# Rests split engine by engine, an earlier low-rank load, thirteen bridging products, and output operands split at their groups

## The chip, the cores and the metric

The kernel runs on one core of one Trainium2 chip. The metric is the device time of one execution in microseconds (us); 904.47 us is the median of three runs of the kernel before (904.07, 904.47, 905.79). A profiled execution of it took 907.22 us, of which 905.4 us are the span that the trace shows. TensorE is called PE here, its weight loads PEld, VectorE DVE, ScalarE ACT, GpSimd POOL and SyncE SP.

## The reference

One encoder block on 512 tokens of width 2048: a normalisation modulated by a condition vector, one input projection whose columns feed two branches, dilated attention with 16 heads and gated linear attention (GLA) with 4 heads, a gate on each, one output projection, the residual and a last normalisation.

```python
mod = jax.nn.silu(c) @ w_cond[layer] + b_cond[layer]
shift, scale, gate = jnp.split(mod, 3, axis=-1)
h = rms_norm(x) * (1.0 + scale[:, None]) + shift[:, None]
proj = h @ w_in[layer]
aq, ak, av, ag, gq, gk, gv, gg, lr_f, lr_b = jnp.split(proj, PROJ_SPLITS, axis=-1)
...
log_g_f = (jax.nn.log_sigmoid((lr_f @ gla_gate_up_fwd[layer] + gla_gate_bias_fwd[layer]).astype(jnp.float32))
           / GLA_GATE_NORM).reshape(ks_)
...
y = jnp.concatenate([a_out, g_out], axis=-1) @ w_out[layer]
x = x + gate[:, None] * y
return rms_norm(x) * final_gain
```

The two low-rank columns `lr_f` and `lr_b` have rank 16 each. Everything is float32.

## The kernel before, in words

Every float32 operand is split into a high and a low part that PE takes at full speed: the high part is a copy by ACT (L493 for weights), the low part the difference by DVE (L477). A product is then three matmuls, high by high, low by high, high by low (`three`, L230 to L232). A weight arrives as a raw tile of 512 KB over SP's queue, is split, and is used.

PE goes through the program in this order. At the start it warms up (`warm`, L296), spreads the condition and warms again (L324) until the first product of stage a (`first_products`, L591) has its operands; stage a and stage b project the modulated tokens. From 187 to 440 us four units (qk2, qk4, qk6, gk) run with the attention of 16 heads beside them. A head has four tiles: `score` (two matmuls L839 and L840, the maximum on DVE L847, the exp on ACT L851, the reciprocal on DVE L854, a scaling on POOL L864), `turn` (transposes L882, the high part `pth` by ACT L888, the low part `ptl` by DVE L889), then `rest` for the edges that lie in 32 rows each (transpose L899, four copies by ACT L906, four differences by DVE L908) and `values` (L915: four matmuls with the high parts, then those with the low parts; its result goes to `oh` and `cat`, L922 and L926). A unit V (440 to 540 us) makes the GLA values by seven products of halves and holds the low-rank product and GLA head 0, whose output blocks `go` (L1123) read the masked scores `at` (L1108); four units for gates (ag0, ag1, gg0, gg1) hold heads 1 to 3. The output projection (744 to 897 us) is two pairs of seven products P1, P7, P6, P4, P5, P3, P2 of halves, each in four groups of weights. Their operands are sums and differences of the parts of `cat` (`to_s1`, `to_s2`, `to_s4`, L1471 to L1477) and their splits `c_h`, `c_l` (`halves`, L1458 and L1459). Some weights are sums of two raw tiles, added by DVE (L466).

The order on PE is written by hand: a unit places pieces of other work at given fractions of its length (the numbers beside a function, such as 0.7 or GLA_FIRST). The other engines take their instructions in the order that a scheduler makes of the program's order and of priorities; `tc.issue_after(x)` keeps a piece behind x. Every engine and each queue works in order, so an instruction that waits holds up what is behind it. A tile from a pool has a number of buffers, and a load into it waits until an old one is free: raw tiles of the output come from a pool of 3 (L396), raw V tiles (L391) wait for the buffer of a weight that has been split.

The low-rank weight `lrb` (256 KB) is loaded behind the unit gk (L1303), copied by ACT (L1306) and split by DVE (L1307) to `lrs`; the second factor `ups` is split at L1326.

Of the kernel before, what the change touches and what calls it, by code (L numbers as in the profile page):

```python
# [10 lines left out]
F32 = mybir.dt.float32  # L11
# [107 lines left out]
TOKENS = [slice(256 * c + a, 256 * c + 256, 2) for a in range(2) for c in range(2)]  # L119

GLA_AT = (0.01, 0.02, 0.33, 0.46, 0.46, 0.56, 0.64, 0.76, 0.76, 0.88)
GLA_FIRST = (0.3, 0.38, 0.55, 0.62, 0.775, 0.81, 0.86, 0.9, 0.92, 0.97)

SUMS_IN = {"ag0": 8, "ag1": 8, "gg0": 8}

# [66 lines left out]
def block_kernel(ctx: ExitStack, tc: tile.TileContext, a: dict):  # L192
# [15 lines left out]
    def T2(name, dt=F32, parts=P):  # L208
        return t2.tile([parts, 512], dt, tag="t2", name=name)
# [83 lines left out]
    def warm(n):  # L293

        for _ in range(n):
            mm(psw, hot[:, :P], hot, start=True, stop=True)  # L296
# [4 lines left out]
    with tc.manual_schedule(engines=PLANNED):  # L301
        small_inputs()
        cond_load(0, 0)
        half_load(0)
        x_load(0)
        half_load(1)
        nc.scalar.preload_act_table_set("silu_and_others")
        nc.vector.memset(hot.bitcast(F32), 1.0)
        nc.vector.memset(epst, EPS)
        nc.vector.memset(ch.bitcast(F32), 0.0)  # L310
        nc.vector.memset(sel.bitcast(F32), 0.0)
        nc.gpsimd.memset(cl.bitcast(F32), 0.0)
        warm(5)

        nc.vector.tensor_copy(ch[:4], cin[:, :512])
        act(sel[:4], cin[:, 512:], AF.Copy)
        tt(cl[:4], cin[:, :512], ch[:4].bitcast(F32), op=ALU.subtract)

        nc.vector.tensor_scalar(bcond[:, 16:32], bcond[:, 16:32], 1.0, None, op0=ALU.add)
        for j in range(4):  # L320
            spread(j, ch, True)
            spread(j, cl, False)
            act(sb[:, 512 * j:512 * j + 512], pcs[j], AF.Silu)
        warm(6)  # L324

    def cond_sum(dst, w, with_, init):

# [65 lines left out]

    def out_tile(s, name):
        if s % 2 and s >= OUT_DEEP:
            return op.tile([P, 2, 512], F32, tag="raw", bufs=3, name=name)  # L396
        return RAW(name, [2, 512])

    second = {}
# [418 lines left out]
    def attention(pairs):  # L818
# [77 lines left out]
        def rest(h):  # L896

            pk = PJ(f"r{h}")
            nc.tensor.transpose(pk[:, :P], pr_.pop((h, 0))[:, 0:128], ident)  # L899
            hi, lo = pts  # L900
            to = [(hi, 0, hi, 32), (hi, 0, lo, 0), (hi, 96, lo, 96), (hi, 64, hi, 96)]
            parts = [(t[a:a + 32, REST_OF[i], :], u[b:b + 32, REST_OF[i], :], pk[96 - 32 * i:128 - 32 * i, :P])
                     for i, (t, a, u, b) in enumerate(to)]
            for pair in (parts[:2], parts[2:]):
                for up, _, of in pair:
                    act(up, of, AF.Copy)  # L906
                for up, low_, of in pair:
                    tt(low_, of, up.bitcast(F32), op=ALU.subtract)  # L908

        def values(h):  # L910
            def go():
# [379 lines left out]
        for q in range(2):  # L1291
            qk_evict(p + 2 + q, ps[2 * q], ps[2 * q + 1])

    ps = unit("gk", False, attention((6, 7)))
    kp_.close()
    gs = mid.enter_context(tc.tile_pool(name="gs", bufs=1, reuse_waits="tile"))
    gla["k"] = B8("gkt", [4, 512])
# [1 line left out]
        act(gla["k"][:, i, :], ps[i], AF.Copy)  # L1299


    lrb = T2("lrb")
    nc.sync.dma_start(lrb.rearrange("p (k c) -> p k c", k=KT), a["w_lr"][0])  # L1303
    lrs = gp.tile([P, KT, 2, 32], F32R, tag="g", name="lrs")
    lrb3 = lrb.rearrange("p (k c) -> p k c", k=KT)
    act(lrs[:, :, 0, :], lrb3, AF.Copy)  # L1306
    tt(lrs[:, :, 1, :], lrb3, lrs[:, :, 0, :].bitcast(F32), op=ALU.subtract)  # L1307
    plr = PA("plr")
# [161 lines left out]
    def to_s1(z):  # L1470
        tt(part(z, 1), part(2 + z, 1), part(z, 1), op=ALU.subtract)  # L1471
# [9 lines left out]
            (0.65, lambda: to_s1(0)), (0.8, lambda: to_s2(0))]  # L1481
    ps = unit("gg1", False, side + some_sums("gg1"))
    gate_evict(ps, cat[3], "g1")
    to_s1(1)
    to_s2(1)
    mid.close()
    op = ctx.enter_context(tc.tile_pool(name="op", bufs=1, reuse_waits="tile"))
    for e in "hl":
# [145 lines left out]
    def later(pair, prod, g, go):  # L1634
        todo.setdefault((pair, prod, g), []).append(go)

    def product(pair, prod, ps, first, last, rows=(0, 1)):

        ah, al = ops[with_[prod]]
        for g in range(4):  # L1640
            s = (pair * len(OUT_ORDER) + OUT_ORDER.index(prod)) * 4 + g
            i0 = gi["O", s]
            ahead = 0 in rows
            if ahead:
                split_hi(i0)
                split_hi(i0 + 1)
                for n in (2, 3, 4, 5):
                    fetch(i0 + n)
                whole(i0 + 2)
                split_lo(i0)  # L1650
                for go in todo.get((pair, prod, g), ()):
                    go()
            wh, wl = wts[i0]
            for n in rows:
                t = slice(P * n, P * n + P)
                for kk in range(2):
                    k = 2 * g + kk
                    c = slice(512 * kk, 512 * kk + 512)
                    three(ps[n], ah[:, k, t], al[:, k, t], wh[:, c], wl[:, c],
                          first and k == 0, last and k == 7, not first)  # L1660
                if ahead and n == 0:
                    split_lo(i0 + 1)

    def a12():
        operand("A12", [B8(f"A12{e}", [4, 512], F32R) for e in "hl"])

    for z in range(2):
        later(0, "P1", 2 * z, halves("S2", z, part(z, 0)))
        later(0, "P7", 2 * z, halves("A22", z, part(2 + z, 1)))
        later(0, "P6", 2 * z, halves("S1", z, part(z, 1)))  # L1670
        later(0, "P6", 2 * z + 1, lambda z=z: (to_s4(z), halves("S4", z, part(z, 0))()))
    later(0, "P4", 0, a12)
    for z in range(2):
        later(0, "P4", 1 + 2 * z, lambda z=z: halves("A12", z, part(2 + z, 0))())
# [133 lines left out]
```

## Time and profile before

| what | us |
|---|---|
| runs, median (lowest, highest) | 904.47 (904.07, 905.79) |
| profiled execution | 907.22 |
| its span | 905.4 |
| PE busy in the span | 890.0 (98%) |
| DVE busy | 731.2 (81%) |
| ACT busy | 491.6 (54%) |
| POOL busy | 125.9 (14%) |
| DMA read from and written to memory, over the span | 305 GB/s |

A row of the timeline gives the start in the span, the time, the engine, the line, the operation, what it writes and reads, and in brackets how long the engine had been idle before it and what ended that. Matmuls overlap, so a matmul of 0.39 us does not hold up the next for as long; the starts tell the pace. The row of a DMA on SP is its issue, not its landing.

### The profile page before, as it was taken

How to read it: one execution, taken by the hardware profiler on the slowest of the kernel's cores; microseconds unless marked ns; L12 is line 12 of the kernel's file. 1: busy time of each engine (PE TensorE's matmuls, PEld its weight loads, DVE VectorE, ACT ScalarE, POOL GpSimd, SP SyncE). 2: the span in 40 equal slices, each digit the busy share in tenths (PEclk: the TensorE clock that was granted, in tenths of full speed). 3: DMA queues.
4: the chain of work that ended last, by engine and by line, in shares of the span. 5: the costliest groups of instructions: out<-in, count | busy, mean ns of one | idle time of the engine just before them, and what ended most of it. 6: DMA issues, size and time to landing. Idle time of an engine off the chain costs nothing.

```text
span 905.4 us, 12339 instructions
## 1 busy us (share of the span) xinstructions
PE 890.0 (98%) x4159; PEld 739.2 (82%) x4159; DVE 731.2 (81%) x1220; ACT 491.6 (54%) x841; POOL 125.9 (14%) x219
## 2 busy tenths in 40 slices
PE   8999999999999999999999999999999999999996
PEld 6888788888888888887778888888888888888885
DVE  7998799878989989888568668595787559797687
ACT  5554533466655745655657554373664248455454
POOL 0000000023323333243000101112020100000001
PEclk9999999999999999999999999999999999999999
DMA  9999489398798898998778879778796988777863
GB/s 342 401 411 363 186 344 367 134 306 226 202 266 273 247 265 247 249 298 223 232 260 255 311 206 308 206 249 262 231 279 208 275 286 289 282 288 249 289 238 154
DMA packets 65547, 242.33 MB, mean 268 GB/s; under 512 B 9190, under 2 KB 11526, under 8 KB 55883
## 3 DMA queue, kind: packets, MB, share of 16 engines
q1 hardware_dynamic: 58724, 199.23, 61.5%
q0 software_dynamic: 6464, 42.01, 19.4%
q8 instruction: 33, 0.54, 0.2%
q10 hardware_dynamic: 296, 0.30, 0.1%
q14 instruction: 30, 0.25, 0.1%
HBM read 224.64 MB, written 51.47 MB: 305 GB/s over the span
## 4 chain that ended last, share of the span: by engine, by line
PE 91%; DVE 3%; ACT 2%; DMA 2%; issue 1%; SPq 0%; DVEq 0%; ACTq 0%
PE ps_qk L230 5%; PE ps_qk L232 5%; PE ps_qk L231 5%; PE g L232 4%; PE g L230 4%; PE g L231 4%; PE stb L232 3%; PE stb L231 3%; PE stb L230 3%; PE ps_ag L232 3%; PE ps_ag L230 3%; PE ps_ag L231 3%; PE o L915 3%; PE sta L230 3%; PE sta L231 3%; PE sta L232 3%
## 5 line engine op out<-in xcount | busy, mean ns | idle before, releaser
L864 POOL TENSOR_SCALAR p<-p,st 128x32 f32<-128x32 f32 (+2 forms) x108 | 59.8, 565 | 159.9 <-DVE st L854 91.2
L328 DVE CUSTOM_DVE_ANT_0 cb<-cb,sb,c_bcond 128x2048 f32<-128x2048 f32 (+1 forms) x32 | 73.4, 2295 | 1.9 <-DMA cb<-in_wm 1.6
L851 ACT ACTIVATE p<-p,st 128x416 f32<-128x416 f32 x64 | 41.0, 641 | 49.2 <-DVE st L847 42.3
L429 POOL DMA_DIRECT2D T<-in_w_o x32 | 23.2, 725 | 159.4 <-ACT V2h L493 14.8
L888 ACT ACTIVATE pth<-t 128x384 fp32r<-128x384 f32 x64 | 31.0, 485 | 19.8 <-PE t L882 11.1
L889 DVE TENSOR_TENSOR ptl<-t,pth 128x384 fp32r<-128x384 f32 x64 | 35.2, 551 | 5.2 <-ACT pth L888 3.7
L882 PE MATMUL t<-c_ident,p 128*128 128x128 f32 x192 | 31.3, 272 | 0.0
L882 PEld LDWEIGHTS t<-c_ident,p 128*128 128x128 f32 x192 | 24.3, 139 | 7.9
L847 DVE CUSTOM_DVE_ANT_0 p<-s,g,st 128x256 f32<-128x256 f32 x64 | 27.7, 432 | 1.8
L847 DVE CUSTOM_DVE_ANT_0 p<-s,g 128x160 f32<-128x160 f32 x64 | 23.5, 367 | 4.2 <-PE s L840 3.5
L328 DVE CUSTOM_DVE_ANT_0 rawg<-rawg,crow,gate 128x1024 f32<-128x1024 f32 x16 | 20.4, 1279 | 4.0 <-DMA rawg<-in_wg 4.0
L1581 POOL TENSOR_SCALAR x<-x,rn 128x512 f32<-128x512 f32 x2 | 2.3, 1167 | 148.5 <-ACT rn L1570 148.5
L429 POOL DMA_DIRECT2D T3V<-in_w_gv x8 | 5.5, 687 | 125.1 <-ACT qk21h L493 118.7
L839 PE MATMUL s<-ks,qh 128*128 128x416 f32 x64 | 22.6, 353 | 0.0
L906 ACT ACTIVATE pth<-r 32x128 fp32r<-32x128 f32 x64 | 17.2, 269 | 9.9 <-PE r L899 4.5
L840 PE MATMUL s<-ks,ql 128*128 128x416 f32 x64 | 22.4, 350 | 0.0
L1091 ACT ACTIVATE sq<-st,sc 128x256 f32<-128x256 f32 x24 | 12.2, 506 | 18.6 <-DVE st L1081 10.0
L328 DVE CUSTOM_DVE_ANT_0 rawg<-rawg,crow,c_bcond 128x1024 f32<-128x1024 f32 x16 | 20.3, 1279 | 0.5 <-DVE g L1028 0.5
L429 POOL DMA_DIRECT2D T<-T x16 | 9.1, 571 | 79.9 <-ACT V8h L493 12.9
L915 PE MATMUL o<-pth,vv 128*128 128x512 f32 (+1 forms) x64 | 15.9, 369 | 2.2 <-DVE pth L908 1.1
L466 DVE TENSOR_TENSOR raw_O<-raw_O,raw_P 128x1024 f32<-128x1024 f32 x8 | 9.8, 1225 | 10.1 <-DMA raw_O<-in_w_o 7.8
L568 ACT ACTIVATE h_hi<-xt,shift 128x512 fp32r<-128x512 f32 x16 | 11.5, 721 | 10.3 <-DVE shift L328 9.5
(1661 smaller groups left out, 3151.6 us busy)
## 6 DMA issues: line engine op xcount, KB each, us to landing
cb<-in_wm SPq DMA_DIRECT2D x31, 1024.0 KB, 9.3
T<-in_w_o POOLq DMA_DIRECT2D x32, 512.0 KB, 6.5
rawg<-in_wg SPq DMA_DIRECT2D x32, 512.0 KB, 5.4
raw_O<-in_w_o SPq DMA_DIRECT2D x32, 512.0 KB, 4.6
raw_qk<-in_w_qk SPq DMA_DIRECT2D x24, 512.0 KB, 4.9
raw_O<-T SPq DMA_DIRECT2D x24, 512.0 KB, 5.0
rawb<-in_w_sb SPq DMA_DIRECT2D x16, 512.0 KB, 8.9
rawv<-in_wv SPq DMA_DIRECT2D x16, 512.0 KB, 5.6
```

The source lines that it names most:

```text
L230: mm(ps, lh, rh, start=first, stop=False, skip_group_check=more)
L231: mm(ps, ll, rh, start=False, stop=False, skip_group_check=more)
L232: mm(ps, lh, rl, start=False, stop=last, skip_group_check=more)
L328: return nc.vector.tensor_tensor_reduce(out=w, in0=w, in1=with_, op0=ALU.mult, op1=ALU.add, scale=1.0, scalar=init, accum_out=dst)
L429: move = nc.gpsimd.dma_start(dst, src, max_dma_last_dim=8192, **how).ins
L847: top = nc.vector.tensor_tensor_reduce(out=t[:, lo:hi], in0=ps[:, lo:hi], in1=gt[h][:, at:at + 2 * (hi - lo) - 1:2], op0=ALU.add, op1=ALU.min,
L851: act(t, t, AF.Exp, bias=st[:, 0:1], scale=-1.0, accum_out=st[:, 1:2])
L864: last["pool"] = nc.gpsimd.tensor_scalar(to, of, st[:, 2:3], 1.0, op0=ALU.mult, op1=ALU.mult).ins
L882: nc.tensor.transpose(pk[:, n_ * P:n_ * P + P], t[:, first_ + kt * P:first_ + kt * P + P], ident)
L888: act(hi, src, AF.Copy)
L889: tt(lo, src, hi.bitcast(F32), op=ALU.subtract)
L915: mm(po[:, P * a0:P * a1], vv[h // 4][:, c, h % 4, :], pt[:, at:at + (a1 - a0 - 1) * step + 1:step, :], start=n_ == z == 0, stop=False, sk ...
```

## The change

It has six parts. The second warm-up has 13 matmuls in place of 6. In `rest` ACT makes all four copies before DVE makes the four differences, where before it was two and two. The low-rank load is issued within the unit gk, at 0.7 of its length, and no longer behind it. In the output, `to_s1` and `to_s2` of the second half are moved from before the output into the groups 2 and 3 of P1, and the sums and splits of the operands are placed in the order of the weights' splits by the new function `in_turn`; the split of S2 goes to group 1 of P1 and of P7 from groups 0 and 2 of P1. The pool of raw tiles in the output has four buffers. Two of the numbers of GLA_FIRST, 0.9 and 0.92, are 0.91 and 0.93.

```diff
@@ -119,7 +119,7 @@
 TOKENS = [slice(256 * c + a, 256 * c + 256, 2) for a in range(2) for c in range(2)]
 
 GLA_AT = (0.01, 0.02, 0.33, 0.46, 0.46, 0.56, 0.64, 0.76, 0.76, 0.88)
-GLA_FIRST = (0.3, 0.38, 0.55, 0.62, 0.775, 0.81, 0.86, 0.9, 0.92, 0.97)
+GLA_FIRST = (0.3, 0.38, 0.55, 0.62, 0.775, 0.81, 0.86, 0.91, 0.93, 0.97)
 
 SUMS_IN = {"ag0": 8, "ag1": 8, "gg0": 8}
 
@@ -321,7 +321,7 @@
             spread(j, ch, True)
             spread(j, cl, False)
             act(sb[:, 512 * j:512 * j + 512], pcs[j], AF.Silu)
-        warm(6)
+        warm(13)
 
     def cond_sum(dst, w, with_, init):
 
@@ -393,7 +393,7 @@
 
     def out_tile(s, name):
         if s % 2 and s >= OUT_DEEP:
-            return op.tile([P, 2, 512], F32, tag="raw", bufs=3, name=name)
+            return op.tile([P, 2, 512], F32, tag="raw", bufs=4, name=name)
         return RAW(name, [2, 512])
 
     second = {}
@@ -901,11 +901,10 @@
             to = [(hi, 0, hi, 32), (hi, 0, lo, 0), (hi, 96, lo, 96), (hi, 64, hi, 96)]
             parts = [(t[a:a + 32, REST_OF[i], :], u[b:b + 32, REST_OF[i], :], pk[96 - 32 * i:128 - 32 * i, :P])
                      for i, (t, a, u, b) in enumerate(to)]
-            for pair in (parts[:2], parts[2:]):
-                for up, _, of in pair:
-                    act(up, of, AF.Copy)
-                for up, low_, of in pair:
-                    tt(low_, of, up.bitcast(F32), op=ALU.subtract)
+            for up, _, of in parts:
+                act(up, of, AF.Copy)
+            for up, low_, of in parts:
+                tt(low_, of, up.bitcast(F32), op=ALU.subtract)
 
         def values(h):
             def go():
@@ -1291,7 +1290,13 @@
         for q in range(2):
             qk_evict(p + 2 + q, ps[2 * q], ps[2 * q + 1])
 
-    ps = unit("gk", False, attention((6, 7)))
+    lrb = []
+
+    def lr_load():
+        lrb.append(T2("lrb"))
+        nc.sync.dma_start(lrb[0].rearrange("p (k c) -> p k c", k=KT), a["w_lr"][0])
+
+    ps = unit("gk", False, attention((6, 7)) + [(0.7, lr_load)])
     kp_.close()
     gs = mid.enter_context(tc.tile_pool(name="gs", bufs=1, reuse_waits="tile"))
     gla["k"] = B8("gkt", [4, 512])
@@ -1299,10 +1304,8 @@
         act(gla["k"][:, i, :], ps[i], AF.Copy)
 
 
-    lrb = T2("lrb")
-    nc.sync.dma_start(lrb.rearrange("p (k c) -> p k c", k=KT), a["w_lr"][0])
     lrs = gp.tile([P, KT, 2, 32], F32R, tag="g", name="lrs")
-    lrb3 = lrb.rearrange("p (k c) -> p k c", k=KT)
+    lrb3 = lrb[0].rearrange("p (k c) -> p k c", k=KT)
     act(lrs[:, :, 0, :], lrb3, AF.Copy)
     tt(lrs[:, :, 1, :], lrb3, lrs[:, :, 0, :].bitcast(F32), op=ALU.subtract)
     plr = PA("plr")
@@ -1481,8 +1484,6 @@
             (0.65, lambda: to_s1(0)), (0.8, lambda: to_s2(0))]
     ps = unit("gg1", False, side + some_sums("gg1"))
     gate_evict(ps, cat[3], "g1")
-    to_s1(1)
-    to_s2(1)
     mid.close()
     op = ctx.enter_context(tc.tile_pool(name="op", bufs=1, reuse_waits="tile"))
     for e in "hl":
@@ -1633,6 +1634,14 @@
 
     def later(pair, prod, g, go):
         todo.setdefault((pair, prod, g), []).append(go)
+
+    def in_turn(pair, prod, g, *fns):
+
+        def go():
+            with tc.issue_after(last["hi"]), tc.issue_after(last["lo"]):
+                for fn in fns:
+                    fn()
+        later(pair, prod, g, go)
 
     def product(pair, prod, ps, first, last, rows=(0, 1)):
 
@@ -1664,11 +1673,13 @@
     def a12():
         operand("A12", [B8(f"A12{e}", [4, 512], F32R) for e in "hl"])
 
+    in_turn(0, "P1", 2, lambda: to_s1(1))
+    in_turn(0, "P1", 3, lambda: to_s2(1))
     for z in range(2):
-        later(0, "P1", 2 * z, halves("S2", z, part(z, 0)))
-        later(0, "P7", 2 * z, halves("A22", z, part(2 + z, 1)))
-        later(0, "P6", 2 * z, halves("S1", z, part(z, 1)))
-        later(0, "P6", 2 * z + 1, lambda z=z: (to_s4(z), halves("S4", z, part(z, 0))()))
+        in_turn(0, ("P1", "P7")[z], 1, halves("S2", z, part(z, 0)))
+        in_turn(0, "P7", 2 * z, halves("A22", z, part(2 + z, 1)))
+        in_turn(0, "P6", 2 * z, halves("S1", z, part(z, 1)))
+        in_turn(0, "P6", 2 * z + 1, lambda z=z: to_s4(z), halves("S4", z, part(z, 0)))
     later(0, "P4", 0, a12)
     for z in range(2):
         later(0, "P4", 1 + 2 * z, lambda z=z: halves("A12", z, part(2 + z, 0))())
```

On DVE, around the rest of attention head 13 (`r` is its transposed tile; L908 in the old and L907 in the new are its differences, `t` a turned tile, `gk7l` the low part of the last weight of the unit gk). Before:

```order
L908 TENSOR_TENSOR pth<-r_4040,pth 32x128
L908 TENSOR_TENSOR ptl<-r_4040,pth 32x128
L889 TENSOR_TENSOR ptl<-t_4050,pth 128x3x128
L847 ISA p_4063,st_4064<-s_4060,g_3867 128x160
L847 ISA st_4064 128x1
L477 TENSOR_TENSOR gk7l<-raw_gk_3978,gk7h 128x1024
L847 ISA p_4063,st_4064<-s_4060,g_3867,st_4064 128x256
L847 ISA st_4064 128x1
L908 TENSOR_TENSOR ptl<-r_4040,pth 32x128
L1243 TENSOR_TENSOR S_4001<-S_4001,h_lo 128x512
L908 TENSOR_TENSOR pth<-r_4040,pth 32x128
```

Now (the first of the four L907 stands three rows further up):

```order
L907 TENSOR_TENSOR ptl<-r_4047,pth 32x128
L847 ISA p_4070,st_4071<-s_4067,g_3874,st_4071 128x256
L847 ISA st_4071 128x1
L907 TENSOR_TENSOR ptl<-r_4047,pth 32x128
L1242 TENSOR_TENSOR S_4008<-S_4008,h_lo 128x512
L907 TENSOR_TENSOR pth<-r_4047,pth 32x128
L854 RECIPROCAL st_4071<-st_4071 128x1
L889 TENSOR_TENSOR ptl<-t_4057,pth 128x3x128
L847 ISA p_4102,st_4103<-s_4099,g_3874 128x256
L847 ISA st_4103 128x1
L477 TENSOR_TENSOR gk7l<-raw_gk_3985,gk7h 128x1024
```

The turn's L889 and the split gk7l stood ahead of the last two differences and stand behind them now.

On ACT, the copy `lrs` and what stands around it, before at the end of head 15:

```order
L1299 ACTIVATE gkt<-ps_gk_3671 128x512
L888 ACTIVATE pth<-t_4277 128x3x128
L1299 ACTIVATE gkt<-ps_gk_3672 128x512
L888 ACTIVATE pth<-t_4286 128x3x128
L906 ACTIVATE pth<-r_4296 32x128 x2
L1306 ACTIVATE lrs<-lrb 128x16x32
L888 ACTIVATE pth<-t_4306 128x3x128
L906 ACTIVATE pth<-r_4296 32x128 x2
```

and now at the first tile of head 15, whose exp is the L851 behind it:

```order
L921 ACTIVATE oh_4127<-o_4115 64x512
L888 ACTIVATE pth<-t_4138 128x3x128
L1309 ACTIVATE lrs<-lrb 128x16x32
L851 ACTIVATE p_4152,st_4153<-p_4152,st_4153 128x416
L888 ACTIVATE pth<-t_4171 128x3x128
L493 ACTIVATE V0h<-raw_V_4083 128x1024
```

The copy has moved from between two turns of the last head to a place 35 rows further up, ahead of an exp, and on SP the load stands between the raw V tiles 4 and 5.

On DVE at the beginning of the output (`O2l` is the low part of the third weight, `c_l` that of an operand). Before:

```order
L1202 TENSOR_TENSOR cat_5990<-cat_5990,sgg_6774 128x512
L1202 TENSOR_TENSOR cat_5990<-cat_5990,sgg_6777 128x512
L1202 TENSOR_TENSOR cat_5990<-cat_5990,sgg_6780 128x512
L1459 TENSOR_TENSOR c_l<-cat_1611,c_h 128x1024
L1202 TENSOR_TENSOR cat_5990<-cat_5990,sgg_6783 128x512
L1477 TENSOR_TENSOR cat_1611<-cat_5127,cat_1611 128x4x256
L1471 TENSOR_TENSOR cat_3027<-cat_5990,cat_3027 128x4x256
L477 TENSOR_TENSOR O2l<-raw_O_6807,O2h 128x1024
```

Now:

```order
L1201 TENSOR_TENSOR cat_5997<-cat_5997,sgg_6781 128x512
L1201 TENSOR_TENSOR cat_5997<-cat_5997,sgg_6784 128x512
L1201 TENSOR_TENSOR cat_5997<-cat_5997,sgg_6787 128x512
L1201 TENSOR_TENSOR cat_5997<-cat_5997,sgg_6790 128x512
L477 TENSOR_TENSOR O2l<-raw_O_6812,O2h 128x1024
L1462 TENSOR_TENSOR c_l<-cat_1618,c_h 128x1024
L1474 TENSOR_TENSOR cat_3034<-cat_5997,cat_3034 128x4x256
L477 TENSOR_TENSOR O3l<-raw_O_6814,O3h 128x1024
```

The third weight's low part stands ahead of the operand's low part and of the sums, of which one (the old L1477) has gone behind the low parts of weights 4 to 9.

## The prediction

> **What bounds the kernel now.** I read the waits of TensorE (PE) first: what it waited for, us in total, times, longest.
>
> ```profile
> PE sta L591 <- ACT h_hi L534: 2.7, 1, 2.7
> ...
> PE o L915 <- DVE pth L908: 1.1, 1, 1.1
> PE o L915 <- ACT pth L888: 1.0, 1, 1.0
> ```
>
> PE sets the time, and what an edit elsewhere can bring is one of these few waits, some tenths that hide between matmuls, or a slow clock. So I looked for clock next, in the table of stretches (length, busy us of PE, of its weight loads, DVE, ACT, POOL, then the clock granted, DMA share, GB/s):
>
> ```profile
> 7.86:11.28 3.42, 1.03 (x5) 0.84 (x6) 2.82 (x6) 2.23 (x5) 0.00 (x0) 1.00 1.03 406
> 11.28:14.69 3.41, 3.41 (x10) 2.64 (x9) 2.31 (x3) 1.00 (x2) 0.00 (x0) 0.50 1.03 429
> ...
> 895.33:898.74 3.41, 1.59 (x7) 0.97 (x6) 2.31 (x6) 2.23 (x6) 0.99 (x1) 1.00 0.26 102
> 898.74:902.15 3.41, 0.00 (x0) 0.00 (x0) 2.10 (x5) 2.01 (x6) 0.00 (x0) 1.00 0.78 310
> ```
>
> After a stretch in which PE was busy for 30% (1.03 of 3.42) the clock was half for 3.41 us. After one of 47% (1.59 of 3.41, at the end) it stayed full. So the 2.7 us wait of the start costs a second time: 3.41 us at half clock lose about 1.7 us of matmuls.
>
> Each wait below is read from starts: a matmul of 512 columns starts 0.23 us after the one before it while nothing holds it up, as the rows of 790.67 and 791.13 show further down, two starts apart.
>
> **The change, part by part.** *Seven more matmuls at the start.* Six stand there and fill nothing that is on the path. Thirteen last 7 x 0.23 = 1.6 us longer, and the hole is 2.7 us, so the first product still waits only for its operand; about 1.1 us stay idle. In the worst place of a 3.41 us stretch PE is then busy for (3.41 - 1.1)/3.41 = 68%, over the 47% that kept the clock. What is late next is the split operands:
>
> ```profile
> 21.20 0.74 DVE L537 SCALAR_TENSOR_TENSOR h_lo<-xt,scale,h_hi 128x512 fp32r<-128x512 f32 x1
> ...
> 23.10 0.39 PE L231 MATMUL sta<-sa2hi,h_lo 128*128 128x512 f32 x1
> ```
>
> This low half is ready at 21.94 and used at 23.10, so of 1.7 us at most 1.15 survive. Against the profiled execution the edit is worth 1.1. Against the median it is worth less if the stretches lie otherwise there. The hole is 2.65 us; if a stretch needs between 1.8 us of it (busy 47%) and 2.4 us (busy 30%) to lose the clock, and stretches of 3.41 us begin anywhere, between (0.76 + 2 x 0.25)/3.41 = 37% and (0.76 + 2 x 0.85)/3.41 = 72% of the executions pay. About half: 0.55. Bounds 0 and 1.1.
>
> [...]
>
> *The rests engine by engine.* In head 13 the DVE rows are (start, us):
>
> ```profile
> 413.74 0.29 DVE L908 TENSOR_TENSOR pth<-r,pth 32x128 fp32r<-32x128 f32 x1 [0.17 <-ACT pth L906]
> ...
> 414.36 0.56 DVE L889 TENSOR_TENSOR ptl<-t,pth 128x384 fp32r<-128x384 f32 x1
> ...
> 415.20 1.22 DVE L477 TENSOR_TENSOR gk7l<-raw_gk,gk7h 128x1024 fp32r<-128x1024 f32 x1
> ...
> 417.89 0.28 DVE L908 TENSOR_TENSOR pth<-r,pth 32x128 fp32r<-32x128 f32 x1
> ```
>
> ```profile
> 416.82 0.40 PE L232 MATMUL ps_gk<-h_lo,gk5h 128*128 128x512 f32 x1
> 418.32 1.05 PE L915 MATMUL o<-pth,vv 128*128 128x512 f32 x4 [1.10 <-DVE pth L908]
> ```
>
> PE was free at 417.05 and started at 418.32, 0.15 behind the last L908 (its end, 418.17): 1.27 lost. In the new order the L889 and the split gk7l stand behind all four L908. The four copies of ACT now come first, two of them more at 0.28 each, so the first L908 goes from 413.74 to 414.3; two L908 take 0.6; from 414.36 to 418.17 it took 3.8, less 0.56 and 1.22 that moved behind, 2.0. The last ends at 416.9 to 417.1, PE starts at 417.1 to 417.25, and **1.05 of the 1.27 is gained**. Behind it queue L889, needed only by the low products some 0.9 us later, and gk7l, which now ends near 414.3 + 2.6 + 0.56 + 0.5 + 1.22 = 419.3 (one score piece of 0.5 ahead of it) in place of 416.4. The other heads have no such wait, and the same 0.57 of delay costs them at most a tenth each; I take 0 for these.
>
> *The low-rank load.* Now (SP, ACT, PE):
>
> ```profile
> 434.49 0.64 SPq L1303 DMA_DIRECT2D lrb<-in_w_lr  x1
> ```
> ```profile
> 435.91 0.60 ACT L1299 ACTIVATE gkt<-ps_gk 128x512 f32<-128x512 f32 x1
> ...
> 437.78 0.55 ACT L906 ACTIVATE pth<-r 32x128 fp32r<-32x128 f32 x2
> 441.12 0.63 ACT L1306 ACTIVATE lrs<-lrb 128x512 fp32r<-128x512 f32 x1 [2.78 <-DMA lrb<-in_w_lr]
> 441.77 0.49 ACT L888 ACTIVATE pth<-t 128x384 fp32r<-128x384 f32 x1
> ...
> 443.36 1.05 ACT L1326 ACTIVATE ups<-upr 128x1024 fp32r<-128x1024 f32 x1
> ```
> ```profile
> 440.92 0.39 PE L232 MATMUL ps_gv_P<-V0l,h_hi 128*128 128x512 f32 x1
> 442.31 1.13 PE L915 MATMUL o<-pth,vv 128*128 128x512 f32 x4 [1.01 <-ACT pth L888]
> ```
>
> The copy lrs holds the last turn of head 15 on ACT, and PE, free at 441.15, starts 1.16 later. With lrs gone from there, ACT has from 435.91 on two gkt (0.5 each by their starts), three L888 (0.49), the four copies (1.1) and ups (1.05), which moves ahead: 4.6 us, to 440.5. That is before 441.15, so the wait ends; a further 0.1 goes in the low products behind it. **1.2 gained.**
>
> But lrs needs a new place. On SP the load stands behind the fourth raw V tile, which waits for the buffer of gk7l: 419.3, with its own issue of 0.64 about 419.9. It is moved past three loads and a store there; the raw V tile now behind it goes 0.64 later, far ahead of its use. On ACT lrs stands between the turn of head 14's second tile and the exp of head 15's first. When does it land? Nearest rows (KB, us from issue to landing), the load itself as it was, and a raw V tile alone, from the stretch 419 to 427:
>
> ```profile
> lrb<-in_w_lr SPq DMA_DIRECT2D x1, 256.0 KB, 6.6
> ```
> ```profile
> raw_V<-in_w_gv SPq DMA_DIRECT2D x1, 512.0 KB, 3.1
> ```
>
> So 423.0 to 426.5. The stretch is quieter than the one at 434, but a tile of 512 KB goes out just ahead: I take 424.0. The exp behind it waits for its maximum:
>
> ```profile
> 423.60 0.48 DVE L847 CUSTOM_DVE_ANT_0 p<-s,g,st 128x256 f32<-128x256 f32 x1
> ```
> ```profile
> 424.00:429.00 5.00, 5.00 (x28) 4.24 (x27) 4.90 (x15) 3.66 (x9) 0.61 (x1) 1.00 0.58 187
> ```
>
> That maximum is there at 424.08, so lrs (0.63) costs ACT nothing if the load lands by 423.45, and each microsecond later delays exp, reciprocal, turn and the next score by as much. And DVE has no room here, 4.90 of 5.00 busy: its half of lrs (0.69, as long as its 128x512 kin at 417) and the wait for two more copies of ACT (0.57) are not hidden: 1.26. At 424.0 the price is 1.26 + 0.55 = **1.8 lost**, at PE's turns and scores of head 15's last tiles. Bounds: 0.7 (early, and PE's slack of about half a microsecond there used) and 1.26 + 3.05 = 4.3.
>
> *The outputs of GLA head 0 one product later.*
>
> ```profile
> 524.30 0.69 DVE L1108 SCALAR_TENSOR_TENSOR at<-c_ident,at 128x512 f32<-128x512 f32 x1
> ```
> ```profile
> 524.46 0.39 PE L232 MATMUL ps_gv_P<-V25l,vS 128*128 128x512 f32 x1
> 525.13 0.46 PE L1123 MATMUL go<-at,gv 128*128 128x128 f32 x2 [0.28 <-ACT V27h L493]
> ```
>
> PE, free at 524.69, waits for `at`, which ends at 524.99 and is taken at 525.13: 0.44. Three matmuls more ahead of it (0.68) cover that. What is later next is the rest of head 0's chain, so I take **0.35 gained** between 0 and 0.5.
>
> *The output's operands at their groups, and a fourth raw tile.*
>
> ```profile
> 744.87 1.23 DVE L1459 TENSOR_TENSOR c_l<-cat,c_h 128x1024 fp32r<-128x1024 f32 x1 [0.90 <-ACT c_h L1458]
> ...
> 746.61 1.22 DVE L1477 TENSOR_TENSOR cat<-cat,cat 128x1024 f32<-128x1024 f32 x1
> 747.75 1.22 DVE L1471 TENSOR_TENSOR cat<-cat,cat 128x1024 f32<-128x1024 f32 x1
> 748.88 1.22 DVE L477 TENSOR_TENSOR O2l<-raw_O,O2h 128x1024 fp32r<-128x1024 f32 x1
> ```
> ```profile
> 749.63 0.39 PE L231 MATMUL g<-O2h,A11l 128*128 128x512 f32 x1
> 750.15 0.50 PE L232 MATMUL g<-O2l,A11h 128*128 128x512 f32 x1
> ```
>
> PE reaches O2l's product at 749.86 and starts at 750.15, and 0.1 more goes right behind: 0.4. In the new order O2l stands ahead of the first three rows, over 3 us earlier. **0.4 gained.** The moved work, two halves c_l and an addition of 1.2 each, comes up again between 771 and 791, where DVE has room only because it waits for a tile:
>
> ```profile
> 782.53 1.22 DVE L466 TENSOR_TENSOR raw_O<-raw_O,raw_P 128x1024 f32<-128x1024 f32 x1 [3.17 <-DMA raw_O<-in_w_o]
> ...
> 789.35 1.22 DVE L477 TENSOR_TENSOR O17l<-raw_O,O17h 128x1024 fp32r<-128x1024 f32 x1
> ```
> ```profile
> 790.67 0.39 PE L230 MATMUL g<-O17h,c_h 128*128 128x512 f32 x1
> ...
> 791.13 0.39 PE L232 MATMUL g<-O17l,c_h 128*128 128x512 f32 x1
> ```
>
> O17l ends 0.56 before its use. The hole of 3.17 us at 782.5 takes two of the three pieces; the third, and two additions that now stand ahead of O17l, must find the tiles earlier, which the fourth raw tile allows. I cost it at nothing; if that cover fails, one piece of 1.2 less 0.56 is 0.7 lost, and all three are 3.1.
>
> **The sum.** 1.05 + 1.2 + 0.35 + 0.4 - 1.8 = 1.2 gained, and the start 0.55 against the median, 1.1 against the profiled execution. That one took 907.22 us, 905.4 in the span and 1.8 around it, 2.75 over the median of 904.47; by the sum it becomes 904.9. The median becomes 904.47 - 1.75 = **902.7 us**.
>
> **Rivals.** *The load lands late.* The gains without it are 3.0, so the whole change is slower from the moment when 1.26 + (landing - 423.45) exceeds 3.0: landing after 425.2. With its old 6.6 us it lands at 426.5: 4.3 lost, 905.8 with nothing from the start, 905.2 with its half. The old row speaks for it, the 3.1 of the raw tile against. Over 427 it is slower by 1.8.
>
> *The start in full, and an early load.* If the median runs had the half clock and the load lands by 423: 3.0 - 0.7 + 1.1 = 3.4, **901.1**. For it: the three runs lie 1.7 us apart, about what the half clock costs.
>
> *The start brings nothing:* the runs of the median had full clock anyway, and 904.47 - 1.2 = **903.3**. For it: the profiled execution, which had half clock, is the slowest of all. [...]
>
> *A new wait in the output.* O17l stands behind two additions that wait for tiles: 0.7 to 3.1 lost, **904.6** in the middle (1.9). For it: the hole is a DMA wait, not spare time. Against: one more tile to fetch ahead.
>
> **How the numbers follow.** A measurement of this kernel tells 0.2%, 1.8 us, from no change: faster is below 902.66. The forecast (load between 423 and 425, the start by half) has 0.42, half of it on either side of that limit: 0.22 faster, 0.20 same. Full start and early load 0.20, faster. No start 0.14: 0.03 faster, 0.11 same. Late load 0.13: 0.08 same, 0.05 slower. New output wait 0.11: 0.06 same, 0.05 slower; it takes the remainder of reorderings that I can't price. Sum: faster 0.45, same 0.45, slower 0.10; I move 0.02 from same to slower since the order of DVE changes in hundreds of rows. The range goes from 900.0 (all bounds on the good side: 3.0 - 0.7 + 1.1 + the 0.15 of GLA and a microsecond for tiles that come earlier) to 905.6 (late load, half start, 0.4 over).
>
> **What would show it.** Clock 1.00 throughout from 5 us on, and no half stretch; if the first half low operand is then waited for at 21.9, the 1.15 holds. No wait over 0.3 us at the o of heads 13 and 15, none at go and at O2l's product. In exchange waits of some 1.8 us in all at turns and scores of head 15 between 424 and 431, and lrs on ACT near 424. Wrong would be: lrb landing past 425.5, a wait at O15l to O20l near 780 to 795, or a wait of the same size at head 13's o, which would mean that the four L908 still stand behind other work on DVE.

## The result

The changed kernel takes 906.44 us (median of 14 runs, 905.90 to 907.75), the kernel before in the same comparison 905.11 us (14 runs, 904.07 to 908.57). The ratio is 1.0016, 95% interval 1.0009 to 1.0023: the change makes it slower by about 1.4 us. The forecast was 902.7 us in a range of 900.0 to 905.6. It has the wrong sign, and the time lies outside the range.

The profiled executions tell the opposite at first sight: 906.70 us with a span of 904.9, against 907.22 with 905.4. Both readings are right, since the profiled execution of the kernel before was 2.1 us longer than its median and that of the changed one only 0.26. What follows has to account for both.

### The profile page after: what moved, and what is told of

It is laid out like the page before. It is cut to its first block, busy times and chain, and to the rows that moved or that the text cites. A ratio compares the mean times of both kernels' runs of the same rounds, so it can differ in the third digit from the quotient of the medians.

```text
span 904.9 us, 12332 instructions
## 1 busy us (share of the span) xinstructions
PE 891.7 (99%) x4166; PEld 739.2 (82%) x4166; DVE 730.7 (81%) x1220; ACT 491.7 (54%) x841; POOL 126.7 (14%) x219
## 4 chain that ended last, share of the span: by engine, by line
PE 48%; DVE 3%; ACT 1%; issue 1%; DMA 1%; DVEq 0%; SPq 0%; ACTq 0%
PE g L231 4%; PE g L232 4%; PE g L230 4%; PE ps_ag L230 3%; PE ps_ag L231 3%; PE ps_ag L232 3%; PE ps_gv_P L231 3%; PE ps_gv_P L230 3%; PE ps_gv_P L232 3%; PE ps_gg L232 2%; PE ps_gg L231 2%; PE ps_gg L230 2%; PE go L1122 2%; PE gx L231 2%; PE gx L232 2%; PE gx L230 2%
## 5 line engine op out<-in xcount | busy, mean ns | idle before, releaser
L851 ACT ACTIVATE p<-p,st 128x416 f32<-128x416 f32 x64 | 41.0, 641 | 56.6 <-DVE st L847 44.8
L889 DVE TENSOR_TENSOR ptl<-t,pth 128x384 fp32r<-128x384 f32 x64 | 35.0, 550 | 3.1 <-ACT pth L888 2.3
L847 DVE CUSTOM_DVE_ANT_0 p<-s,g,st 128x256 f32<-128x256 f32 x64 | 27.6, 432 | 1.7
L847 DVE CUSTOM_DVE_ANT_0 p<-s,g 128x160 f32<-128x160 f32 x64 | 23.6, 369 | 4.5 <-PE s L840 3.8
L839 PEld LDWEIGHTS s<-ks,qh 128*128 128x128 f32 x64 | 12.0, 188 | 7.7 <-issue 1.9
L1358 DVE TENSOR_TENSOR vS<-rawS,vS 128x1024 fp32r<-128x1024 f32 x8 | 9.7, 1223 | 9.5 <-ACT vS L1357 9.4
```

Source lines behind the costliest of these rows:

```text
L839: mm(ps[:, :NK], qh[:, q], ks[:, k], start=True, stop=False)
L847: top = nc.vector.tensor_tensor_reduce(out=t[:, lo:hi], in0=ps[:, lo:hi], in1=gt[h][:, at:at + 2 * (hi - lo) - 1:2], op0=ALU.add, op1=ALU.min,
L851: act(t, t, AF.Exp, bias=st[:, 0:1], scale=-1.0, accum_out=st[:, 1:2])
L889: tt(lo, src, hi.bitcast(F32), op=ALU.subtract)
```

## The profile after

The waits of TensorE (PE) in the changed kernel (us in total, times, longest):

```profile
PE s L839 <- DVE st L847: 1.8, 4, 1.0
PE warm L296 <- DVE hot L308: 1.5, 1, 1.5
PE sta L591 <- ACT h_hi L534: 0.7, 1, 0.7
PE t L882 <- DVE st L847: 0.5, 1, 0.5
```

The waits of the old list that the change aimed at are gone or shorter: the 2.7 us at the start are 0.7, and the two at `o` and the one at `go` don't appear. In their place stands a wait that the old list does not have: scores `s`, and one turn `t`, that wait for the maximum on DVE (L847).

The start, in the table of stretches (length, busy us of PE, PEld, DVE, ACT, POOL, the clock granted, DMA share, GB/s):

```profile
7.86:11.28 3.42, 2.70 (x12) 1.89 (x12) 2.46 (x7) 2.32 (x5) 0.00 (x0) 1.00 1.02 414
11.28:14.69 3.41, 3.41 (x17) 2.83 (x16) 2.60 (x3) 0.96 (x3) 0.00 (x0) 1.00 1.04 431
```

The half clock after the hole is gone: from 11.28 to 14.69 us the clock granted is 1.00, where the trace of before has 0.50. Where the two traces stand at the same matmul tells what each part did. The table gives the start of one matmul in both, counted from the end of PE's list, where the same matmuls stand:

| place | before | after | after less before |
|---|---|---|---|
| early in the attention units | 202.51 | 201.23 | -1.28 |
| in unit qk6 | 364.08 | 363.76 | -0.32 |
| in unit gk, before head 13's end | 405.01 | 405.26 | +0.25 |
| in unit V, attention done | 447.65 | 448.04 | +0.39 |
| in unit ag0 | 574.82 | 574.75 | -0.07 |
| output | 760.75 | 760.23 | -0.52 |
| last matmul | 896.53 | 896.00 | -0.53 |

The start brings 1.28 us in these two traces. The attention up to 405 us loses 1.53 of it, where I had forecast nothing at all. From 405 to 448 gains and losses nearly cancel. GLA gives 0.46 and the beginning of the output 0.45, as forecast.

What happens at a score is seen at a score in unit qk6, behind the rest of the head before it. Before (DVE, then PE):

```profile
365.36 0.55 DVE L889 TENSOR_TENSOR ptl<-t,pth 128x384 fp32r<-128x384 f32 x1
...
366.56 0.48 DVE L847 CUSTOM_DVE_ANT_0 p<-s,g,st 128x256 f32<-128x256 f32 x1
```
```profile
366.45 0.40 PE L232 MATMUL ps_qk<-h_lo,qk66h 128*128 128x512 f32 x1
366.69 0.35 PE L839 MATMUL s<-ks,qh 128*128 128x416 f32 x1
```

After:

```profile
366.16 0.48 DVE L847 CUSTOM_DVE_ANT_0 p<-s,g,st 128x256 f32<-128x256 f32 x1
...
367.17 0.55 DVE L889 TENSOR_TENSOR ptl<-t,pth 128x384 fp32r<-128x384 f32 x1
```
```profile
366.13 0.40 PE L232 MATMUL ps_qk<-h_lo,qk66h 128*128 128x512 f32 x1
366.80 0.43 PE L839 MATMUL s<-ks,qh 128*128 128x416 f32 x1 [0.27 <-DVE st L847]
```

A score needs a buffer that an earlier tile has left: the tiles `s` of the scores and `t` of the turns share a pool of three (L218). Before, the turn's L889 ended at 365.91 and left one, 0.8 us ahead of the score. Now L889 stands behind the four differences of the rest and ends at 367.7; the first to leave a buffer is L847 at 366.64, and the score starts at 366.80 where the pace would have it at 366.36. L847 itself is not late: it starts 0.40 us earlier than before, L889 1.81 later. The same is seen before other scores: 0.20, 0.17, 0.44, 0.14, 0.44 and 0.39 us above the pace at 211, 225, 275, 303, 367 and 417 us, 1.8 in sum where before there were 0.13.

The low-rank load (ACT, DVE, PE) in the changed kernel:

```profile
425.30 0.63 ACT L1309 ACTIVATE lrs<-lrb 128x512 fp32r<-128x512 f32 x1 [3.04 <-DMA lrb<-in_w_lr]
425.83 0.63 ACT L851 ACTIVATE p<-p,st 128x416 f32<-128x416 f32 x1
```
```profile
426.59 0.17 DVE L854 RECIPROCAL st<-st 128x1 f32<-128x1 f32 x1 [1.58 <-ACT p L851]
426.67 0.67 DVE L1310 TENSOR_TENSOR lrs<-lrb,lrs 128x512 fp32r<-128x512 f32 x1
```
```profile
429.73 0.52 PE L882 MATMUL t<-c_ident,p 128*128 128x128 f32 x3 [0.54 <-DVE st L847]
...
432.68 0.42 PE L839 MATMUL s<-ks,qh 128*128 128x416 f32 x1 [1.03 <-DVE st L847]
```

ACT waits 3.04 us for the load with an exp behind it; the reciprocal on DVE waits 1.58 for that exp, and the turn and the next score of head 15 come late, 0.70 and 1.20 us above the pace. That is a price of 1.9 in this trace, which the forecast had put at 1.8. The load was issued on SP at 420.48 and its copy began at 425.30 (forecast: issue 419.9, landing 424.0).

## The experiments

Each run is compared with runs of the kernel before on the same chip, whose medians were 905.67, 905.52 and 905.43 us in the three groups below (29, 33 and 15 runs, each group on another chip). The first four kernels are the first group.

**The bridging matmuls alone**, those of the second warm-up.

```diff
-        warm(6)
+        warm(13)
```

> The kernel before with thirteen bridging matmuls and nothing else. Theory A: the timed executions of the kernel before keep the full clock at the start and only its profiled execution fell into a half stretch; then the time stays within 0.3 us of before, though this kernel's trace shows no half clock. Rival B: most timed executions of before pay the half stretch; then it is 1.1 us faster (ratio 0.9988) and its clock column stands 0.002 above that of before.

904.93 us against 905.67, ratio 1.0000 (0.9991 to 1.0008). No gain that can be measured, though the medians lie 0.74 us apart: theory A. The interval leaves out the 1.1 us of rival B (0.9988), but not the 0.55 of the forecast (0.9994). The granted clock of the single runs points the same way. In the second group 27 of 33 runs of the kernel before have a mean clock of 0.997 or 0.998, and only 6 have 0.996 or less; these 6 are at 906.28 to 910.48 us, the others at 904.09 to 906.55. In the other two groups 6 of 29 and 3 of 15 have 0.996 or less, and there they lie among the others (904.31 to 908.75 and 904.46 to 906.34 us). So the half stretch that the profiled execution showed seems to be paid by about one execution in five. The mean clock is only a rough sign of it: with thirteen matmuls 2 of the 14 runs of the change and 1 of the 11 here have 0.996 as well. The reason is in the traces of the kernels that also have six matmuls, here that of the rests alone:

```profile
7.86:11.28 3.42, 1.82 (x9) 1.16 (x8) 2.69 (x6) 2.31 (x6) 0.00 (x0) 1.00 1.03 415
11.28:14.69 3.41, 3.41 (x17) 2.80 (x16) 2.60 (x3) 1.16 (x3) 0.00 (x0) 1.00 1.04 431
```

Its hole was 1.6 us and lies whole in the first of these stretches, PE was busy for 53%, and the clock granted stayed at 1.00. The hole is not a constant 2.65 us: it was 1.6 here, 1.7 in the trace of the early load alone and 1.1 in that of the output's parts alone (3.42 less 1.82, 1.76 and 2.31 us busy). The pace ahead of it varied too. In the trace of before the products that spread the condition (L299), just ahead of the second warm-up, start 0.23 us apart from 4.70 us on, in that of the change from 5.15 on and 0.42 apart until then. In the trace of before the second warm-up ended at 7.60 us, whereas in the three others with six matmuls PE is busy for all of 4.45 to 7.86, with 14 matmuls in it with the early load alone and 11 in the other two. So of these four traces the hole was longest in the one whose second warm-up was over by 7.86 us.

The trace of the bridging matmuls alone had a second surprise, in the row of the copy lrs with the load where it always was:

```profile
437.63 0.63 ACT L1306 ACTIVATE lrs<-lrb 128x512 fp32r<-128x512 f32 x1 [1.21 <-DMA lrb<-in_w_lr]
```

ACT waited 1.21 us and not 2.78, and there was no wait at the `o` of head 15. The load took 5.0 us from issue to landing there, and 6.6 in the trace of before. So the 1.2 us at that place are not in every execution.

**The rests alone.**

```diff
-            for pair in (parts[:2], parts[2:]):
-                for up, _, of in pair:
-                    act(up, of, AF.Copy)
-                for up, low_, of in pair:
-                    tt(low_, of, up.bitcast(F32), op=ALU.subtract)
+            for up, _, of in parts:
+                act(up, of, AF.Copy)
+            for up, low_, of in parts:
+                tt(low_, of, up.bitcast(F32), op=ALU.subtract)
```

> The kernel before with the rests split engine by engine and nothing else. Theory A: the new waits of TensorE at the scores of heads 2 to 14 come from this edit, since the maximum that frees the score's buffer now stands behind differences that wait for four copies; expected are waits at the scores of 1.3 to 1.6 us in all, o of head 13 down from 1.27 to 0.2, o of head 15 down from 1.2 to nothing because the scheduler now puts the low-rank copy behind the last turn even with the load where it was: in sum 0.9 us faster. Rival B: the score waits come from the earlier load or other parts; then none over 0.2 us here, and 2.3 us faster.

905.68 us, ratio 1.0005 (0.9996 to 1.0013): no gain. The trace shows the waits of theory A: scores 2.0 us above the pace (0.21, 0.20, 0.44, 0.14, 0.45, 0.44, 0.14), `o` of head 13 at 0.20, and no wait at the `o` of head 15, because the copy lrs now stands behind the last turn and behind a weight's copy although the load was not moved. What theory A holds to be late, the maximum L847, is not: by the rows at 366 us it is L889. The expected gain of 0.9 did not come in the time; the interval goes to 0.4 at most. Part of that is the 1.2 us of head 15, which the kernel before doesn't always lose. One more wait was in this trace that the trace of before had not, in the second half of the output (PE, DVE):

```profile
861.36 0.50 PE L232 MATMUL gx<-O43l,c_h 128*128 128x512 f32 x1 [0.45 <-DVE O43l L477]
```
```profile
858.95 1.23 DVE L466 TENSOR_TENSOR raw_O<-raw_O,raw_P 128x1024 f32<-128x1024 f32 x1 [1.12 <-DMA raw_P<-in_w_o]
```

It is a late raw tile, 0.61 us above the pace. The wait is 0.36 in the trace of the early load alone and 0.73 in that without bridging matmuls, so it stands in three of the five traces with three raw tiles, and in none of those with four.

**The change without the early load.**

```diff
-    lrb = []
-
-    def lr_load():
-        lrb.append(T2("lrb"))
-        nc.sync.dma_start(lrb[0].rearrange("p (k c) -> p k c", k=KT), a["w_lr"][0])
-
-    ps = unit("gk", False, attention((6, 7)) + [(0.7, lr_load)])
+    ps = unit("gk", False, attention((6, 7)))
...
+    lrb = T2("lrb")
+    nc.sync.dma_start(lrb.rearrange("p (k c) -> p k c", k=KT), a["w_lr"][0])
```

> The changed kernel with the low-rank load back behind the unit gk. Theory A: the waits at the turn and the score of head 15 (0.70 and 1.20 us) are the price of the load's new place, and the wait at o of head 15 stays away without it, since the rests' order alone moves the copy: 1.9 us faster than the changed kernel, 0.6 faster than before. Rival B: the wait at o of head 15 comes back with 1.2: 0.7 faster than the changed kernel, 0.6 slower than before.

904.86 us, ratio 0.9991 (0.9981 to 1.0002), against 1.0016 of the whole change: 0.0025, about 2.3 us less. Theory A. Head 15 has no wait but 0.14 at one score, and the `o` of head 15 is clear without the early load. So in this change the load's new place costs 1.9 us and brings nothing: what it should bring, the rests' order had brought already.

**Rests in heads 13 and 15 alone, load where it was, all other parts as in the change.**

```diff
-            for pair in (parts[:2], parts[2:]):
+            for pair in ((parts,) if h in (13, 15) else (parts[:2], parts[2:])):
```

> Thirteen bridging matmuls, the output's operands, the fourth raw tile and the later GLA outputs as in the change; the rests split engine by engine in heads 13 and 15 alone; the load where it was. Theory A: no wait at scores beyond those of before, none over 0.25 us at o of heads 13 and 15, none at go and at O2l: 1.08 + 1.28 + 0.45 + 0.4 = 3.2 us less than before without the start, ratio 0.9965. Rival B: the score waits are not from the rests of the other heads: they stay, and the gain is 1.8.

902.56 us, ratio 0.9970 (0.9958 to 0.9982): 2.7 us faster than before, and faster than the kernel above, which differs from it in the rests of the other 14 heads, by 1.9 us in the ratios and 2.3 in the medians. Theory A: those rests are the price. PE's list of waits has two lines left, both at the start, and ACT at the end of head 15 shows the copy lrs behind all that `o` needs:

```profile
PE warm L296 <- DVE hot L308: 1.5, 1, 1.5
PE sta L591 <- ACT h_hi L534: 0.7, 2, 0.5
```
```profile
435.77 1.11 ACT L906 ACTIVATE pth<-r 32x128 fp32r<-32x128 f32 x4
436.91 0.49 ACT L888 ACTIVATE pth<-t 128x384 fp32r<-128x384 f32 x1
437.67 0.63 ACT L1306 ACTIVATE lrs<-lrb 128x512 fp32r<-128x512 f32 x1 [0.27 <-DMA lrb<-in_w_lr]
```

By the starts one score is still 0.28 us late, at 415 us: it stands just ahead of the `o` of head 13, so it is the price of that head's own rest.

**The change with the split of the low-rank weight held back.** The load stays as early; this and the next three are the second group.

```diff
-                    act(hi, src, AF.Copy)
-                    tt(lo, src, hi.bitcast(F32), op=ALU.subtract)
+                    last["turn_hi"] = act(hi, src, AF.Copy).ins
+                    last["turn_lo"] = tt(lo, src, hi.bitcast(F32), op=ALU.subtract).ins
...
-    act(lrs[:, :, 0, :], lrb3, AF.Copy)
-    tt(lrs[:, :, 1, :], lrb3, lrs[:, :, 0, :].bitcast(F32), op=ALU.subtract)
+    with tc.issue_after(last["turn_hi"]), tc.issue_after(last["turn_lo"]):
+        act(lrs[:, :, 0, :], lrb3, AF.Copy)
+        tt(lrs[:, :, 1, :], lrb3, lrs[:, :, 0, :].bitcast(F32), op=ALU.subtract)
```

> The changed kernel with the low-rank load as early as in the change, but its copy and its difference held behind the last turn of head 15. Theory A: the 1.9 us at the turn and the score of head 15 come from the copy's place on ACT, where it waits for the load ahead of an exp; then both waits fall to 0.15 or less, the o of head 15 stays clear, and the kernel is 1.9 us faster than the changed one (ratio to before 0.9993). Rival B: the early load itself delays raw V tiles and scores: waits of 1 us or more stay in head 15 (ratio 1.001).

904.65 us, ratio 0.9992 (0.9983 to 1.0001). Theory A: the waits of 0.70 and 1.20 are gone, 0.13 is left at one score, and the time is that of the change without the early load. The transfer itself costs nothing that can be measured; the place of the split on ACT and DVE does. The edit holds back both, so which of the two engines makes the price is not shown.

**The early load alone.** The edit is the one on the load in the change, on the kernel before.

> The kernel before with the early low-rank load alone. Here the split of the last gk weight stays early, so the load is issued near 417 us and not at 420.5, and lands near 422. Theory A: the price hangs on the landing; before 423.5 it costs 0.3 us or less at head 15, the old wait at its o (up to 1.2) goes, and the kernel is 0 to 0.9 us faster than before. Rival B: the work of 0.63 and 0.69 us on ACT and DVE is the price wherever it lands: waits of 1 us or more between 424 and 433, and the kernel is no faster.

904.42 us, ratio 0.9991 (0.9983 to 1.0000): about 0.8 us faster, though the interval ends at no gain; theory A. The load was issued at 417.11, because the split of the last gk weight, whose buffer is waited for, stands earlier with the old rests, and the copy on ACT stands ahead of a weight's copy and not of an exp:

```profile
423.43 0.63 ACT L1310 ACTIVATE lrs<-lrb 128x512 fp32r<-128x512 f32 x1 [2.03 <-DMA lrb<-in_w_lr]
```

Head 15 loses 0.28 us at one transpose, and its `o` is clear. By the traces the same edit costs 1.9 us with the new rests and 0.3 with the old ones. Whether the earlier landing (423.4 against 425.3) or the other neighbours on ACT and DVE make more of that difference, no run here separates.

**The output's parts, four raw tiles and the GLA outputs alone.** The edits are those of the change on GLA_FIRST, the pool and the output.

> The kernel before with the output's operands at their groups, four raw tiles and the later GLA outputs. Theory A: the waits at go (0.44) and at O2l (0.4) go and nothing takes their place: 0.85 us faster, ratio 0.9991. Rival B: the moved work on DVE makes a wait at one of O15l to O20l of 0.7 us or more: no faster than before. The wait at o of head 15 is looked at too: it was 1.17 in the trace of before and 0 in that of thirteen matmuls alone, so it should come out anywhere between.

904.09 us, ratio 0.9983 (0.9974 to 0.9992), 1.5 us faster. The waits at go and O2l are gone and nothing took their place: theory A, with more gain than the 0.85 expected, though the interval reaches that. The wait at O43l, which some traces with three raw tiles have and this one, with four, hasn't, may be the rest; that was not tried alone. The wait at the `o` of head 15 was 0.84 us above the pace here:

```profile
438.96 0.63 ACT L1306 ACTIVATE lrs<-lrb 128x512 fp32r<-128x512 f32 x1 [2.45 <-DMA lrb<-in_w_lr]
```
```profile
440.16 1.14 PE L915 MATMUL o<-pth,vv 128*128 128x512 f32 x4 [0.68 <-ACT pth L888]
```

**No bridging matmuls.**

```diff
-        warm(6)
+        warm(0)
```

> The kernel before without the six bridging matmuls. TensorE then idles some 4 us at the start, so a half stretch comes in every execution and not in some. Theory A: each execution loses what the profiled one of before lost there, 1.1 to 1.3 us: the median stands 1 us over that of before, with a clock column of 0.996 or less in nearly all runs. Rival B: the operands of stage a come late enough to hide it: the clock column falls by 0.002, the time stays within 0.3 us.

906.11 us, ratio 1.0007 (0.9996 to 1.0019). All 11 runs have a mean clock of 0.995 or 0.996, where 27 of the 33 runs of the kernel before beside them have 0.997 or 0.998. So the half stretch seems to come in every execution, as expected. The trace has it from 9.30 to 12.71 us (worked out from a granted clock of 0.71 over 7.86 to 11.28 and of 0.79 over 11.28 to 14.69), behind a stretch in which PE was busy for 0.97 of 3.41 us; its hole was 3.0 us and not some 4. Its price is some 0.6 us, between nothing and 1.7: the interval does not decide between the two theories.

**The rests behind the turn.** The held-back split as above, and in each head the copies and differences of the rest behind those of the last turn. This and the next two are the third group.

```diff
-                if i == 3:
-                    rest(h)
+                behind = rest(h) if i == 3 else None
...
+                if behind:
+                    behind()
```

> The late split of the low-rank weight, and in every head the four copies and four differences of the rest behind the copy and the difference of the last turn, where the change has them ahead. Theory A: the score waits come from the buffer that the turn's difference frees: in the change it stands behind the four differences. With it ahead again the score waits of 2.1 us in all fall below 0.5, and waits at the o of several heads come in their place, since o needs the last difference: 1 us or more at head 13. Rival B: the score waits come from the four copies on ACT being in one piece; then they stay at 1.5 us or more.

905.21 us, ratio 0.9997 (0.9987 to 1.0006). Theory A: the score waits are gone, and the waits went to `o`:

```profile
PE o L917 <- DVE pth L909: 2.0, 5, 0.7
```

Above the pace they are 0.35, 0.54, 0.82, 0.57, 0.24 and 0.54 us at six heads, 3.1 in sum. At head 13 it was 0.54 and not the expected 1 or more. The buffer that L889 frees is what the scores waited for. With the rest in one piece either the score or `o` waits, according to what stands first on DVE; in the trace of before, with the rest in two pairs, there were 0.26 and 0.18 at two `o` and 0.13 at one score, besides head 13.

**The faster kernel again, and with the early load.** The first is the kernel with the rests in heads 13 and 15 alone; the second adds the early load with the split held back.

> The same kernel as the one with the rests split in heads 13 and 15 alone, once more beside the others: ratio to before 0.996 to 0.998, no wait over 0.3 us between 200 and 750 us.

> The rests split in heads 13 and 15 alone, thirteen bridging matmuls, the output's and GLA's parts, and the low-rank load early with its split behind the last turn. Theory A: with o of head 15 clear already by the order, the early load has nothing left to give: within 0.4 us of the kernel with the load where it was. Rival B: ACT's wait for the old load still delays something; then 0.5 us or more faster than that.

902.73 us and 902.71 us, both with ratio 0.9963 (0.9951 to 0.9976). The first confirms the gain, some 3 us; one score wait of 0.30 us stands at 414.6. The early load adds nothing to it: theory A. What the rests of heads 13 and 15 gain was not tried alone: the ratios 0.9970 and 0.9963 against the 0.9983 of the output's parts leave 1.2 to 1.8 us for them and the thirteen matmuls together, from different groups and with intervals that overlap.

## Why the prediction was wrong

Step by step, in the order of its sum:

- **Bridging, 0.55 (bounds 0 and 1.1).** The mechanism is right in the traces: no half stretch (granted clock 1.00 from 11.28 to 14.69 us), 1.28 us earlier in the attention than the profiled execution of before. For the median the runs show none of it (alone: 1.0000, 0.9991 to 1.0008), though that interval does not exclude 0.55. The weak step is "about half" of the executions pay. It took the hole of 2.65 us for a constant and let only the place of the stretches vary. The hole itself varied, from 1.1 to 2.65 us over four traces, and was longest in the trace whose second warm-up ended first; with the holes of 1.1 to 1.7 us the clock granted was 1.00 from 4.45 to 14.69 us. Of the 77 runs of before in the three groups 15 had a mean clock of 0.996 or less. That stretches of 3.41 us begin anywhere, and that their busy share decides on the clock, was my estimate from one trace; no run shows it. At the start the half clock began at 11.28 us in the trace of before and at 9.30 in that without bridging matmuls.
- **Rests, head 13, 1.05.** Right at `o`: 1.27 us above the pace before, 0.19 after. The score ahead of it takes back 0.39, which the sum did not have.
- **Rests, the other heads, 0.** This is the step that failed most, "the same 0.57 of delay costs them at most a tenth each; I take 0". A tenth for each of 14 heads is 1.4 us, and the sum had nothing for it. I followed the four differences to `o`, and L889 to its own readers, the low products, which are not in a hurry. I did not give enough weight to its second reader: the buffer that it empties. Five scores waited 0.14 to 0.44 us each, and a sixth, 0.39 at 417 us, behind head 13's own rest. The other heads cost 1.5 us net by the table of starts, and 1.9 to 2.3 us by the comparison of kernels with and without the rests of the 14 heads.
- **`o` of head 15, 1.2 gained.** The wait did go. But the price was taken from one execution: over four traces with the old order the wait was 1.17, 0.84, 0.57 and 0, on average 0.65, as the load took 6.6, 6.3, 6.0 and 5.0 us to land. And the gain was booked to the load. The rests alone clear it.
- **Early load, 1.8 lost.** 1.9 measured. Landing 1.2 us later than taken, the price right by way of two errors that cancel, since by the forecast's own rule a landing at 425.2 would have cost 3.0. The delay behind 423.45 alone is 1.75, so the 1.26 of further work in that rule was hidden for the most part; no run separates the two.
- **GLA, 0.35, and O2l, 0.4.** 0.46 and 0.45 by the starts. The cover that I named for the output held: in the window of O15l to O20l no wait came. O43l's wait of some executions, which no trace with four raw tiles has, I had not seen, since the trace of before has none there.

The account: 1.75 forecast as gain, 1.35 lost, 3.1 apart. The other heads are 1.5 to 2.3 of that, the score ahead of head 13's `o` 0.4, the start up to 0.55, and the part of head 15's wait that the median doesn't have about 0.55. These make 2.4 to 3.8.

The single edits show the same from another side. Their ratios are 1.0000, 1.0005, 0.9991 and 0.9983, together 2.1 parts in a thousand faster; all four in one kernel are 1.6 slower. Two things that lie between them are that the rests and the load both clear the same wait, 0.65 us on average, which counts once, and that the new rests turn the load's price from 0.3 into 1.9 us. They make 2.3 of the 3.3 us; the rest lies within the intervals of the five ratios.

Of the rivals, the late load was nearest in its mechanism: a wait at head 15 in place of the one at its `o`. It had the landing at 426.5 and priced 4.3. The start that brings nothing agrees with the run of the thirteen matmuls alone, within its interval. No rival had the scores.

## What to carry to other kernels

When an instruction is moved back on an engine that works in order, list everything that it releases, the buffer that it empties as well as the value it makes; the reader in a hurry may be the next user of the buffer. A profiled execution is one draw: before a wait that hangs on a load is booked as a gain, look whether other traces of the same code have it. And when two edits clear the same wait, book it once; with several edits in one change, each alone and the whole less one tell which of them pays; here the rests' new order costs time in fourteen heads of sixteen.

## What the runs showed of the hardware

The same load of 256 KB from the same place in the program took 5.0 to 6.6 us from issue to landing over four traces with the old order, and with its arrival a wait of PE went from 0 to 1.17 us.

At the start the clock granted was 0.50 from 11.28 to 14.69 us in the trace of before, behind a stretch (7.86 to 11.28) with PE busy for 1.03 of 3.42 us, 30%. In the trace without bridging matmuls it was half from 9.30 to 12.71, behind 0.97 of 3.41 us, 28%. With 1.76, 1.82 and 2.31 us busy from 7.86 to 11.28 (51%, 53% and 68%, in the traces of the early load, of the rests and of the output's parts alone) it was 1.00 up to 14.69. Near the end of the kernel before it was 1.00 from 898.74 to 902.15 us, behind 1.59 of 3.41 us, 47%. What lies between 30% and 47% is not known from these runs. At half clock four matmuls of 512 columns took 1.69 us from start to start (11.28 to 12.97, before), at full clock 0.90 (17.44 to 18.34). Without bridging matmuls the mean clock was 0.996 or less in all of 11 executions, but the time moved by only 0.0007 (-0.0004 to 0.0019).

A matmul of 512 columns with split operands started 0.23 us after the one before it (790.67 to 791.58 us in the trace of before); of those of 128 columns with operands that are not split, four took 0.45 (525.87 to 526.32), 0.11 each.
